# Full rows, with zeros, for the second product of each attention score, and measured prices for TensorE in the list schedule

## The chip, the cores and the metric

The kernel runs on one core of a Trainium2 chip. The metric is the device time of one execution in microseconds (us). The program is one launch; five engines (PE for matrix products, DVE and ACT for elementwise work, POOL, SP for transfers) each run their own queue in order and wait for one another by semaphores.

## The reference, cut to what matters

Two models stand one behind the other. The first block has two layers, each an attention with two kinds of heads and a gated feed-forward network (FFN). The second block has two layers with a gated linear attention, a softmax attention and a convolution branch; it isn't touched by the change but for its order. What is touched are the scores of the first block, for 256 tokens and 64-wide heads:

```python
# first kind (differential) and second kind (moba, here one block of 256 keys)
logits = jnp.einsum('bqhmd,bkhmd->bmhqk', qblk, k).astype(jnp.float32) * scale + bias
logits = jnp.where(dist >= 0, logits, -jnp.inf)
p = jax.nn.softmax(logits, axis=-1)
...
lo = jnp.einsum('bhqd,bhjd->bhqj', qch, ko).astype(jnp.float32) * scale + bias_o
```

q and k are normalised by their root mean square over the 64 channels of a head. Everything is asked for in float32.

## The kernel before, in words

**Products in parts.** The kernel keeps float32 accuracy with a faster product type by splitting each operand into a high and a low part, and multiplying high by high, high by low and low by high (`mm3`, three products for one). Weights come from HBM as `raw` tiles of 128 x 1024 numbers; ACT makes their high parts `wH`, DVE their low parts `wL`. The wide projections are the bulk of PE's work.

**Attention of the first block.** `attention1` runs four groups in each of two layers: two pairs of the first kind (`diff_pair`), two of the second (`moba_pair`). A group projects q and k for two 128-wide channel tiles, normalises them in `qk_group`, projects v, and then takes the scores in `attn_scores`, once for each of its two channel tiles `a`. A channel tile holds two heads (or two maps of one head) of 64 channels, m = 0 on partitions 0 to 63 and m = 1 on partitions 64 to 127. For token tile t (128 queries) and m there are two products into the same piece of PSUM:

- the first has all 128 rows: `qh` holds the high parts of q twice, on the head's own 64 partitions and, copied by a transfer, on the other 64; `ks` holds the high parts of k on the own partitions and the low parts on the others. One product gives high by high and high by low.
- the second takes the low parts `ql` of q, on the head's own 64 partitions only, by the high parts of k there: 64 rows.

So the eight groups of the two layers have 16 such products each, 64 first and 64 second ones in all. Between them and the transposes of the probabilities stands a chain of DVE and ACT work on `sb`: scale and bias (the bias comes from `strip`, which ACT's queue fetches by transfers in the first layer), maximum, exponential, sums, quotients.

**Order.** All instructions are recorded first (`Rec.record`), each with a price (`Rec.cost`) and a latency. `Rec.order` then simulates the engines with these prices, gives out tile slots, and the instructions are issued, engine by engine, in the order of their simulated starts. The prices decide the order of the whole kernel, not only of the part they speak of. Tiles of 512 numbers for each partition come from a ring "T" of 24 slots (`t2`, `t2r`), those of 1024 from a ring "Q" of 24 slots (`t4`, `t4r`). Ring Q holds the weights on their way (at most 4 `raw`, 7 high, 7 low), modulation weights (at most 4), and `qh` and `ks`.

Of the kernel before, what the change touches and what calls it, by code (L numbers as in the profile page):

```python
# [33 lines left out]
# columns of the packed per-channel parameters  # L34
# [79 lines left out]
# parts of the modulation (layer, part) by the tensor engine, and by the vector engine beside the FFNs and the gates  # L114
# [17 lines left out]
class Rec:  # L132
    """Records instructions, then issues them in the order of a simulated list schedule."""
# [39 lines left out]
    def cost(self, eng, method, out, args, kw):  # L173
        n = self.free(out)
        if eng == "PE":
            if method == "transpose":
                return 109
            lhs = args[1]
            m = self.free(lhs)
            if m <= 64 and self.box(out)[0] > 0:  # L180
                return 27
            if lhs.dtype == F32:
                return 2 * max(107.0, n * 0.8333 + 2)
            return max(107.0, n * 0.4167 + 2)
# [23 lines left out]
    def last(self, ap):  # L208
        """The last instruction that wrote ap's tile."""
        return max(i for _, i, w, _ in self.acc[ap.tensor.name] if w)  # L210

    def record(self, eng, method, fn, args, kw):
# [20 lines left out]
        for ap, w in [(a, False) for a in ins] + [(a, True) for a in outs]:  # L233
# [16 lines left out]
            if bank and eng == "PE" and w and (kw.get("start") or method == "transpose"):  # L250
                c = (b[0], b[1], 0, 1 << 30)   # a first product clears the bank's bits
# [19 lines left out]
    def order(self):  # L271
# [17 lines left out]
        wait = {k: sorted(v, key=lambda t: first[t]) for k, v in ftag.items()}   # tiles without slots  # L289
        held = {k: set() for k in ftag}  # L290
        freeat = {k: [0.0] * self.caps[k] for k in ftag}   # times at which free slots became free
# [3 lines left out]
        future = {e: [] for e in engs}    # (ready, prio, i)  # L295
        avail = {e: [] for e in engs}     # (prio, i)
        parked = {}                       # tag -> ops that wait for a slot
# [9 lines left out]
        def slot_time(o):  # L307
            """When the tiles that o is the first to use can have slots; None: not known yet."""
            t = 0.0
            need = {}  # L310
            for tn in o.new:
                k = self.tiles[tn]
                n = need.get(k, 0)
                fr = freeat[k]
                if len(fr) <= n or not fits(k, tn):
                    return None, k
                t = max(t, sorted(fr)[n])
                need[k] = n + 1
            return t, None

        def fits(k, tn):
            """Whether the tiles that come before tn still find slots, taken in order, when tn has one now."""
# [125 lines left out]
class Emit:  # L448
    def __init__(self, ctx, tc, io):
# [19 lines left out]
        # the tensor engine's clock rises after some time of work  # L469
# [11 lines left out]
        # weights in the order of their use  # L481
# [9 lines left out]
        for l in range(2):  # L491
            seq += [(io["w2r"][l], 1024)]
            seq += [(io["w2"][l * 66 + g], 2048) for g in range(66)]
            if l == 0:   # the output projection: once for the context, once for the latents
                seq += seq[-4:]
# [8 lines left out]
    # ---- small things  # L504
# [38 lines left out]
    # ---- weights: high and low parts of each group, split ahead of their use  # L543
# [28 lines left out]
    def psplit(self, ps, hi, lo):  # L572
        """The parts of what is in PSUM."""
# [4 lines left out]
    def mm3(self, out, w, x, start, stop):  # L578
        """out (+)= w^T x with w = (hi, lo) stationary and x = (hi, lo) moving."""
# [5 lines left out]
    def proj_t(self, out, half, x, cols):  # L585
        """out[n, tok] over the 8 k tiles; half: weights [128, 8, 128]."""
# [4 lines left out]
    def proj_v(self, out, halves, x, tok):  # L591
        """out[tok, n] over the 8 k tiles; halves: two of [128, 4, 256]."""
# [4 lines left out]
    # ---- 1/sqrt(v + eps) of columns [128, n]  # L597
# [23 lines left out]
    def gsum(self, ps, sqs, ones, start=True, stop=True):  # L621
        """Weighted sums of each [128, n] of sqs over its partitions: rows of its group of ps, one after the other."""
# [6 lines left out]
    def gcols(self, ps, ng, n):  # L629
        """The sums of ng groups token by token: a view [128, n // 128, group, row of the group] of PSUM."""  # L630
# [8 lines left out]
    def bcast(self, out, col):  # L639
        """out[:, t] = col[t] on every partition."""  # L640
        self.nc.tensor.transpose(out, col.broadcast_to([P, P]), self.ident)

    def xstat(self, j, src, state, hurry=HURRY):
        """Sums of squares over channels, gathered from channel tile j on; src [128, n]."""
# [16 lines left out]
    def xcols(self, state, n):  # L661
        """Mean squares of n tokens, token by token: columns."""
# [5 lines left out]
    def xrstd(self, state, n):  # L668
        """1/rms of n tokens, on every partition: a PSUM tile [128, n]."""
# [6 lines left out]
    # ---- modulation of the second block  # L676
# [11 lines left out]
    def mod_part(self, l, part, after):  # L688
        """512 of the 3072 modulation channels of layer l."""
# [25 lines left out]
    def mod_open(self, parts):  # L715
        """For parts by the vector engine: the silu of c along the free dimension, doubled, on every partition."""
# [16 lines left out]
    def mod_step(self):  # L733
        """The next 128 of the channels of mod_open's parts."""
# [19 lines left out]
    # ---- first block  # L754
# [13 lines left out]
    def bias_strip(self, i, after):  # L768
        """Biases of the heads 2 i and 2 i + 1 by distance."""
# [10 lines left out]
    def lam(self, l, init):  # L780
# [10 lines left out]
        # -(exp0 - exp1 + init)  # L791
# [4 lines left out]
    def xg(self, j, g, H, L):  # L796
        """The high and low parts of channel tile j of x g, not yet normalised."""
# [17 lines left out]
    def attn_scores(self, pr, a, qg, kn, rq, rcol, head):  # L815
        """Probabilities, not yet normalised, of the two 64-wide parts of channel tile a."""
# [3 lines left out]
        for t in range(2):  # L820
            for m in range(2):
                o = pss[m][:, t * T:(t + 1) * T]
                ms, qs, ks = slice(m * 64, (m + 1) * 64), slice(a * T + t * P, a * T + (t + 1) * P), slice(a * T, (a + 1) * T)
                nc.tensor.matmul(o, qg[0][:, m, qs], kn[:, m, ks], start=True, stop=False)
                nc.tensor.matmul(o, qg[1][ms, qs], kn[ms, m, ks], start=False, stop=True)
# [18 lines left out]
    def attn_transpose(self, a_sb):  # L844
# [5 lines left out]
        # blocks: (q0,k0) (q1,k0) (q1,k1)  # L850
# [3 lines left out]
    def qk_group(self, psq, psk, qscale_g, kg, guard):  # L854
        """Scaled q, normalised k and the columns 1/rms of q for two channel tiles.

        Of each 64 wide part of q its high parts twice, on all partitions, and its low parts; of k the high
        parts on the part's own partitions and the low parts on the others."""
# [10 lines left out]
        qh, ql, ks = self.t4r("qh"), self.t2r("ql"), self.t4r("ks")  # L869
        part = (slice(0, 64), slice(64, P))  # L870
        for m, own in enumerate(part):
            nc.scalar.activation(qh[own, m, :], psq[own], AF.Copy, scale=qscale_g[own])
            nc.sync.dma_start(qh[part[1 - m], m, :].bitcast(F32), qh[own, m, :].bitcast(F32))
            nc.vector.scalar_tensor_tensor(ql[own], psq[own], qscale_g[own], qh[own, m, :].bitcast(F32), ALU.mult, ALU.subtract)
# [14 lines left out]
    def attention1(self, l, H, L, Y, stat):  # L889
# [9 lines left out]
        # of each token: mean square + eps; eps times it, the guard of norms of what is not yet scaled; 1/rms  # L899
# [92 lines left out]
    def ffn(self, l, U, stat0, stat, g1):  # L992
# [6 lines left out]
        def down(i):  # L999
            w = self.nextw(2)  # L1000
            for n in range(KT):
                o = acc[n // 2][:, (n % 2) * T:(n % 2 + 1) * T]
                ns = slice(n * P, (n + 1) * P)
                for q in range(2):
# [3 lines left out]
                    # the first product clears the bits of its whole bank, so that of the other half only writes  # L1008
# [103 lines left out]
    # ---- second block  # L1112
# [21 lines left out]
    def pair_t(self, w, x, nt, nt1=None, parts=((0, 512),)):  # L1134
        """Two n tiles; their PSUM parts [128, nt]."""
# [16 lines left out]
    def group_v(self, w, x, out, order=(0, 1)):  # L1152
        """out [128 tokens, 4 token tiles, 256] for 512 tokens."""
# [6 lines left out]
    def gated(self, ps, n):  # L1160
        """2 silu(ps)."""
# [20 lines left out]
    def split4(self, t, n):  # L1182
        """The parts of t [128, 2, n of 512]."""
# [21 lines left out]
    def context0(self):  # L1205
        """The context's h of the first layer."""
# [9 lines left out]
    def layer2(self, l):  # L1216
# [6 lines left out]
        # decays' low rank part  # L1223
# [3 lines left out]
        # the columns are there twice: the products with the low parts of the second ones make rows of their own  # L1227
        nc.vector.tensor_copy(hi[:, :, 64:], lo[:, :, 64:].bitcast(F32))
        for c0, c1 in parts:
            for k in range(KT):  # L1230
                nc.tensor.matmul(ps[:, c0:c1], hi[:, k, :], h[0][:, k, c0:c1], start=k == 0, stop=k == KT - 1)
                if k < KT - 1:   # the last product has all rows, as the first
                    for q in (k,) if k < KT - 2 else (k, k + 1):
                        nc.tensor.matmul(ps[:64, c0:c1], hi[:, q, :64], h[1][:, q, c0:c1], start=False, stop=False)
        # stacked, for each direction, for one product with the stack of the decays' other factor
# [32 lines left out]
        # output  # L1268
# [22 lines left out]
    def out_last(self, l, O):  # L1291
        """The last output projection, norm and residual, with tokens on partitions."""
# [37 lines left out]
    def out_pass(self, l, s, O):  # L1330
        """Output projection, norm and residual of the latents (s = 0) or the context (s = 1)."""
# [26 lines left out]
    def h_part(self, l, s, rb, H, L):  # L1358
        """h of the latents (s = 0) or the context (s = 1)."""
# [12 lines left out]
    def pair_x(self, w, X, nt):  # L1372
        """Two n tiles of products with the 8 k tiles X."""
# [13 lines left out]
    def gate(self, l, b, X, h, nt, acc, hb, first):  # L1387
        """acc (+)= 2 sigmoid(h w_g + b_g) (X w_br), channel tile by channel tile."""
# [24 lines left out]
    def gla_head(self, l, hd, h, rz, nt):  # L1413
        nc = self.nc
        S = nt // T
        # decays: cumulated logarithms, times 16
# [7 lines left out]
        # rows for the high part, the low part, the high part again (here the low part of the weights), the low rows  # L1424
# [24 lines left out]
        # q, k, v  # L1449
# [12 lines left out]
        # products q k^T with the decays, transposed: slots (s lat0, lat1; t lat), (s ctx0, ctx1; t ctx), (s ctx0, ctx1; t lat)  # L1462
# [20 lines left out]
        for lv in (6, -1, 0, 1, 2, 3, 4, 5):  # L1483
# [6 lines left out]
            if m == 1:  # L1490
                # the factors of k are 1, those of q the single steps
# [5 lines left out]
            else:  # L1497
                # differences to the last of the first half (forward) and the first of the second half (backward)
# [26 lines left out]
        # from the context to the latents, over the state  # L1525
# [23 lines left out]
        # times v  # L1549
# [17 lines left out]
        # gate  # L1567
# [14 lines left out]
    def rope(self, t, n):  # L1582
        """Rotates the 256 latent tokens of t [128, n, 512] in place."""
# [3 lines left out]
        for b in range(4):   # the other halves of the rotated pairs; the signs are with the sines  # L1587
# [30 lines left out]
    def att_qz(self, l, i, h, nt):  # L1618
        """Two heads' q, rotated, not yet normalised; 1/rms; twice the silu of their gates."""
        nc = self.nc  # L1620
        S = nt // T
        if True:
# [10 lines left out]
            # columns: head, token tile  # L1633
# [71 lines left out]
def lay_inputs(inp):  # L1705
# [5 lines left out]
    def tpair(W, c0, c1):  # L1711
        """[128, 2 n tiles, 8 k tiles, 128]"""
# [24 lines left out]
    for l in range(2):  # L1737
# [28 lines left out]
        for part in range(6):  # L1766
            w = W[:, part * 512:(part + 1) * 512]
            if (l, part) in MODPE:   # k by k
                wada.append(w.reshape(KT, P, 512).transpose(1, 0, 2).reshape(P, 4096))
            else:   # channels on partitions  # L1770
# [107 lines left out]
```

## Time and profile before

| | |
|---|---|
| median of 3 runs | 2107.88 us (2101.41 to 2108.41) |
| span of the profiled execution | 2111.4 us |
| PE busy | 2087.5 us, 99% of the span |
| DVE busy | 1466.8 us, 69% |
| ACT busy | 1169.8 us, 55% |
| mean granted clock of PE | 0.985 of full speed |

The profiled execution has no time of its own beside its span, which lies 3.5 us above the median of the runs. Products are pipelined: one of 128 x 256 shows as 0.28 us of busy time, and the next one starts long before it ends. What a product costs PE is therefore read from the starts of its neighbours, not from its busy time.

### The profile page before, as it was taken

To read this page: it belongs to the slowest core of one execution; us is meant where nothing else is said; L and a number is where in the kernel's file an instruction comes from. 1 tells how busy PE (TensorE), PEld (TensorE's weight loads), DVE (VectorE), ACT (ScalarE), POOL (GpSimd) and SP (SyncE) were. 2 spreads that over 40 slices of the span, in tenths; PEclk is the share of its full clock that TensorE was granted. 3 is DMA by queue.
4 is the path that set the end of the run, shared out by engine and by line. 5 is a ranking of instruction groups with operands and counts; after the bars stand their busy time and mean duration, and the time that the engine had idled before them with its cause. 6 is when DMAs were issued, how large, how long until landed. Compare 5 with 4: busy or idle time off the path is not lost.

```text
span 2111.4 us, 35551 instructions
## 1 busy us (share of the span) xinstructions
PE 2087.5 (99%) x14158; PEld 1877.0 (89%) x14158; DVE 1466.8 (69%) x2846; ACT 1169.8 (55%) x2055; POOL 0.2 (0%) x4
## 2 busy tenths in 40 slices
PE   9989999999999999999999999999999999999998
PEld 7769999888999998898888888888887999999997
DVE  6668996676876689995267855554356888697664
ACT  6556555665666586764256423333356786575452
POOL 0000000000000000000000000000000000000000
PEclk9989999989999999999999999999999999999999
DMA  8565665353565512223212443333361224436552
GB/s 280 129 118 176 226 230 187 122 200 124 177 201 186 179 46 75 66 71 107 83 50 81 145 154 120 121 119 120 100 239 52 100 83 160 156 115 199 192 188 70
DMA packets 86846, 292.68 MB, mean 139 GB/s; under 512 B 9452, under 2 KB 17176, under 8 KB 86424
## 3 DMA queue, kind: packets, MB, share of 16 engines
q1 hardware_dynamic: 81544, 281.50, 39.9%
q10 hardware_dynamic: 5136, 8.91, 2.8%
q8 instruction: 111, 1.82, 0.3%
q14 instruction: 55, 0.45, 0.1%
HBM read 282.51 MB, written 4.19 MB: 136 GB/s over the span
## 4 chain that ended last, share of the span: by engine, by line
PE 97%; DMA 1%; DVE 0%; ACT 0%; issue 0%; SPq 0%; ACTq 0%; DVEq 0%
PE mm L442 76%; PE x L442 12%; PE acc L442 6%; PE ms L442 3%; DMA strip<-brow 1%; DMA xx<-in_xt_dram 0%; DVE s L442 0%; ACT h L442 0%; SPq L442 0%; DVE sb L442 0%; ACT wH L442 0%; ACT y L442 0%; ACT xg L442 0%; ACT at L442 0%; DVE h L442 0%
## 5 line engine op out<-in xcount | busy, mean ns | idle before, releaser
L442 DVE TENSOR_TENSOR wL<-raw,wH 128x1024 fp32r<-128x1024 f32 (+1 forms) x472 | 570.3, 1217 | 309.0 <-PE mm L442 146.4
L442 ACT ACTIVATE wH<-raw 128x1024 fp32r<-128x1024 f32 (+1 forms) x472 | 491.5, 1052 | 249.6 <-DVE wL L442 112.4
L442 PE MATMUL mm<-h2H,wH 128*128 128x256 f32 (+1 forms) x1504 | 504.3, 338 | 2.1 <-ACT h2H L442 2.1
L442 PE MATMUL mm<-h2L,wH 128*128 128x512 f32 (+2 forms) x1504 | 503.6, 337 | 0.0
L442 PE MATMUL mm<-h2H,wL 128*128 128x256 f32 (+1 forms) x1472 | 497.8, 338 | 0.0
L442 PEld LDWEIGHTS mm<-h2H,wH 128*128 128x128 f32 x1504 | 283.7, 190 | 33.7 <-issue 3.7
L442 PEld LDWEIGHTS mm<-h2L,wH 128*128 128x128 f32 (+1 forms) x1504 | 283.2, 189 | 28.3 <-issue 1.6
L442 PEld LDWEIGHTS mm<-h2H,wL 128*128 128x128 f32 x1472 | 279.2, 190 | 30.0 <-issue 2.2
L442 PE MATMUL mm<-h,wH 128*128 128x256 f32 x1216 | 219.6, 283 | 0.0
L442 PEld LDWEIGHTS mm<-h,wH 128*128 128x128 f32 x1216 | 189.6, 192 | 0.0
L442 PE MATMUL mm<-h,wL 128*128 128x256 f32 x608 | 171.9, 283 | 0.0
L442 PE MATMUL mm<-xg,wH 128*128 128x256 f32 x704 | 145.0, 304 | 1.9 <-ACT wH L442 1.9
L442 PE MATMUL acc<-hid,wH 128*128 128x256 f32 x704 | 128.2, 283 | 0.0
L442 PEld LDWEIGHTS mm<-xg,wH 128*128 128x128 f32 x704 | 120.3, 209 | 6.2 <-issue 3.1
L442 PEld LDWEIGHTS mm<-h,wL 128*128 128x128 f32 x608 | 116.7, 192 | 0.0
L442 PE MATMUL mm<-xL,wH 128*128 128x512 f32 (+1 forms) x320 | 111.6, 349 | 0.0
L442 PE MATMUL mm<-xH,wL 128*128 128x512 f32 (+1 forms) x320 | 111.2, 348 | 0.0
L442 PE MATMUL mm<-xH,wH 128*128 128x512 f32 (+1 forms) x320 | 111.1, 348 | 0.0
L442 PEld LDWEIGHTS acc<-hid,wH 128*128 128x128 f32 x704 | 109.7, 192 | 0.8 <-issue 0.8
L442 PE MATMUL mm<-xg,wL 128*128 128x256 f32 x352 | 106.3, 304 | 0.4 <-DVE wL L442 0.4
L442 PE MATMUL acc<-hid,wL 128*128 128x256 f32 x352 | 98.5, 283 | 0.0
L442 ACT ACTIVATE gt<-mm,hb 128x512 f32<-128x512 f32 (+1 forms) x48 | 27.8, 580 | 114.9 <-PE mm L442 114.8
(294 smaller groups left out, 3903.2 us busy)
## 6 DMA issues: line engine op xcount, KB each, us to landing
raw<-in_w_dram SPq DMA_DIRECT2D x272, 512.0 KB, 3.8
raw<-in_w1up_dram SPq DMA_DIRECT2D x88, 512.0 KB, 4.2
wada<-in_wada_dram SPq DMA_DIRECT2D x48, 512.0 KB, 5.7
raw<-in_w1in_dram SPq DMA_DIRECT2D x46, 512.0 KB, 5.2
raw<-in_w1dn_dram SPq DMA_DIRECT2D x44, 512.0 KB, 4.2
raw<-in_w1out_dram SPq DMA_DIRECT2D x16, 512.0 KB, 4.3
crow<-in_crow_dram SPq DMA_DIRECT2D x6, 512.0 KB, 6.2
qh<-qh SPq DMA_DIRECT2D x16, 128.0 KB, 2.2
```

The costliest lines, as they stand in the source:

```text
L442: o.fn(*o.args, **o.kw)
```

## The change

Three edits change what is computed or when; the rest of the diff takes comments away.

1. In `qk_group`, `ql` gets its own plane for each m, of 128 partitions x 512 numbers, in a tile of ring Q in place of one of ring T. POOL writes zeros on the other head's 64 partitions of each plane, before DVE writes the low parts on the own 64.
2. In `attn_scores`, the second product reads all 128 rows of `ql` and of `ks`. The zeros meet the low parts of k, so that the sum is the same.
3. In `Rec.cost`, PE's prices change. A product of n columns cost max(107, 0.4167 n + 2) ns and costs max(111, 0.4167 n + 13.3); a float32 one is two passes, each of twice the columns. A product with fewer than 128 rows costs 190 ns more. One with at most 32 output rows costs 110 in any case, where those with at most 64 not at the start of the partitions cost 27.

```diff
@@ Rec.cost
             lhs = args[1]
             m = self.free(lhs)
-            if m <= 64 and self.box(out)[0] > 0:
-                return 27
+            if m <= 32:
+                return 110
+            passes = 1
             if lhs.dtype == F32:
-                return 2 * max(107.0, n * 0.8333 + 2)
-            return max(107.0, n * 0.4167 + 2)
+                n, passes = 2 * n, 2
+            rows = self.box(lhs)[1] - self.box(lhs)[0]
+            return passes * max(111.0, n * 0.4167 + 13.3) + (190 if rows < P else 0)
@@ attn_scores
-                ms, qs, ks = slice(m * 64, (m + 1) * 64), slice(a * T + t * P, a * T + (t + 1) * P), slice(a * T, (a + 1) * T)
+                qs, ks = slice(a * T + t * P, a * T + (t + 1) * P), slice(a * T, (a + 1) * T)
                 nc.tensor.matmul(o, qg[0][:, m, qs], kn[:, m, ks], start=True, stop=False)
-                nc.tensor.matmul(o, qg[1][ms, qs], kn[ms, m, ks], start=False, stop=True)
+                nc.tensor.matmul(o, qg[1][:, m, qs], kn[:, m, ks], start=False, stop=True)
@@ qk_group
-        qh, ql, ks = self.t4r("qh"), self.t2r("ql"), self.t4r("ks")
+        qh, ql, ks = self.t4r("qh"), self.t4r("ql"), self.t4r("ks")
         part = (slice(0, 64), slice(64, P))
+        for m in range(2):
+            nc.gpsimd.memset(ql[part[1 - m], m, :].bitcast(F32), 0.0)
         for m, own in enumerate(part):
             nc.scalar.activation(qh[own, m, :], psq[own], AF.Copy, scale=qscale_g[own])
             nc.sync.dma_start(qh[part[1 - m], m, :].bitcast(F32), qh[own, m, :].bitcast(F32))
-            nc.vector.scalar_tensor_tensor(ql[own], psq[own], qscale_g[own], qh[own, m, :].bitcast(F32), ALU.mult, ALU.subtract)
+            nc.vector.scalar_tensor_tensor(ql[own, m, :], psq[own], qscale_g[own], qh[own, m, :].bitcast(F32), ALU.mult, ALU.subtract)
```

## Rows read from the trace of the kernel before

**Rows 1.** The page: busy time of the engines; shares of the chain that ended last.

```profile
PE 2087.5 (99%) x14158; PEld 1877.0 (89%) x14158; DVE 1466.8 (69%) x2846; ACT 1169.8 (55%) x2055; POOL 0.2 (0%) x4
...
PE 97%; DMA 1%; DVE 0%; ACT 0%; issue 0%; SPq 0%; ACTq 0%; DVEq 0%
```

**Rows 2.** Stretches: length, busy us (instructions) by engine, clock, DMA share, GB/s.

```profile
30.00:165.00 135.00, 127.06 (x780) 102.42 (x780) 86.18 (x233) 70.76 (x160) 0.00 (x0) 0.86 0.65 140
...
530.00:2111.00 1581.00, 1571.12 (x10432) 1417.81 (x10430) 1079.64 (x1960) 857.11 (x1458) 0.00 (x0) 1.00 0.38 125
300.00:320.00 20.00, 20.00 (x169) 20.00 (x169) 18.34 (x28) 12.48 (x17) 0.00 (x0) 1.00 0.76 258
```

**Rows 3.** PE's waits: for whom, us in total, times, longest.

```profile
PE x L442 <- issue: 4.8, 1, 4.8
PE x L442 <- DVE sb L442: 2.6, 2, 2.4
```

**Rows 4.** Timeline of PE around the first score burst: start, us.

```profile
35.30 0.28 PE L442 MATMUL mm<-xg,wH 128*128 128x256 f32 x1
35.42 0.28 PE L442 MATMUL mm<-xg,wL 128*128 128x256 f32 x1
...
36.78 0.39 PE L442 MATMUL x<-ks,qh 128*128 128x256 f32 x1
37.09 0.38 PE L442 MATMUL x<-ks,ql 64*128 64x256 f32 x1
37.41 0.39 PE L442 MATMUL x<-ks,qh 128*128 128x256 f32 x1
...
40.97 0.58 PE L442 MATMUL x<-ks,qh 128*128 128x256 f32 x1
41.48 0.58 PE L442 MATMUL x<-ks,ql 64*128 64x256 f32 x1
...
43.44 0.63 PE L442 MATMUL mm<-xg,wH 128*128 128x256 f32 x2
43.86 0.41 PE L442 MATMUL mm<-xg,wL 128*128 128x256 f32 x1
```

**Rows 5.** The eight score bursts, PE's products of tile ks alone: length, busy, clock.

```profile
108.70:117.75 9.05, 8.04 (x16) 0.50 0.71 24
143.00:147.52 4.52, 4.41 (x16) 1.00 0.80 26
...
498.20:503.23 5.03, 4.91 (x16) 1.00 0.34 106
sum 47.29, PE 45.02; mean PE 5.63
```

**Rows 6.** The first burst, all of PE's products.

```profile
36.15:42.00 5.85, 5.85 (x20) 0.81 0.86 81
```

**Rows 7.** The eight stretches at half clock, all of PE's products.

```profile
39.80:46.60 6.80, 6.80 (x26) 0.50 0.55 93
...
152.40:162.70 10.30, 9.45 (x31) 0.50 0.71 217
...
sum 61.60, PE 60.10; mean PE 7.51
```

**Rows 8.** The same eight stretches, products of tile ks alone.

```profile
sum 61.60, PE 18.00; mean PE 2.25
```

**Rows 9.** Timeline of PE before the third burst; the idle time stands in brackets.

```profile
108.76 0.55 PE L442 MATMUL x<-ks,qh 128*128 128x256 f32 x1 [4.75 <-issue]
```

**Rows 10.** Tile sb's waits (us, times); a row of ACT's timeline.

```profile
  DMA strip<-brow: 8.7, 4
...
95.98 8.67 ACTq L442 DMA_DIRECT2D strip<-brow  x4
```

**Rows 11.** Memsets, of DVE and of POOL.

```profile
L442 DVE MEMSET warm<- 128x512 f32 x1 | 0.5, 485 | 0.1
...
L1868 POOL MEMSET const-float32-0.0<- 128x1 f32 x1 | 0.1, 99 | 0.2 <-issue 0.2
```

## The prediction, made before the changed kernel ran

> **What bounds the kernel.** I read the page first. PE is busy for 99% of the span and carries 97% of the chain that ended last; DVE and ACT are busy for 69% and 55% [rows 1]. So whatever takes PE time counts, unless a wait takes its place. Next the stretches: the two attentions of the first block lie at about 30 to 165 us and 400 to 530 us, and in the first of them the granted clock is 0.86; from 530 us on PE is busy for 1571 of 1581 us at 1.00 [rows 2]. PE's list of waits is short, the longest one 4.8 us [rows 3]. A busy PE isn't a fast one, so I then read starts on the timeline. Two neighbouring projections of 128 x 256 start 0.12 us apart (35.30, 35.42). In the score burst a 128-row product is followed after 0.31 us and a 64-row one after 0.32 us (36.78, 37.09, 37.41), though both have 256 columns too [rows 4]. Last come the stretches at half clock, eight of them, 61.6 us together [rows 7]. The reader should see two costs that the page books as busy time: slow score products, and a clock that falls beside them.
>
> **The padding itself.** A pair of first and second product takes 0.63 us from start to start, where two projections would take 0.24 [rows 4]. The eight bursts hold 45.0 us of score products, 128 in all [rows 5]; at 0.12 us each they would take 15.4. That is 29.6 us, if what costs is the switch between 128 and 64 rows. The count of products is unchanged, and the columns of each also, so nothing is added on PE. The row that bounds it from the other side: were the rows not the cause, the gain is 0.
>
> A page of the Trainium skill speaks on either side here. "TensorEngine Tiling (Array Packing)", Key Properties, says that changing the tiling mode drains the engine; the 0.31 us beside 0.12 agrees. "TensorE: Matmul & The Clock Gate", Why this matters for your kernels, says that a product over few rows takes the same time as one over all 128: by that the padding would give 0 and the sum would be some 30 us less; the 0.31 us disagrees.
>
> **The clock.** In the first burst PE is busy for all of its 5.85 us, and the clock still falls inside it: 0.81 on the mean [rows 6], 0.50 from 39.8 to 46.6 us [rows 7]. Before it fell PE had done nothing but alternate 128 and 64 rows. The projections before the burst, one every 0.12 us, ran at full clock, as those from 300 to 320 us do [rows 2, 4]. With full rows the burst becomes like them, so I expect the clock to stay up. The eight stretches at half clock hold 60.1 us of busy PE. I leave out the one from 152.4 us (9.45 us), where PE had waited. Of the other 50.65 us, 18.0 are score products, already counted [rows 7, 8]. The remaining 32.65 us are projections at 0.21 us each (two between 43.44 and 43.86) in place of 0.12 [rows 4]: at full clock they take 32.65 x 0.12 / 0.21 = 18.65, which saves 14.0. Gross sum: 29.6 + 14.0 = 43.6 us.
>
> The same skill page, The HAM clock gate, ties half clock to an idle engine. By it a burst without a gap would not be the reason, and the 14.0 us would stay lost; the row with 5.85 busy of 5.85 us speaks against that reading.
>
> **What comes back as waits.** Three of the eight places can't give their full share.
> - The third burst begins after a PE gap of 4.75 us [rows 9], with ACT held for 8.67 us by four strip issues just before [rows 10]. Nothing in the change touches these issues. The clock is already at 0.50 through the whole burst [rows 5], and I leave it so: 16 products at 0.21 cost 3.4 us and not 1.9, and some 16 projections behind them lose 0.09 each. Back: 3.0 us.
> - The fourth burst (4.41 us) is the layer's last. After it PE runs out of projections and waits for the softmax chain, itself held by late strips for up to 8.7 us [rows 5, 10]. What the burst saves, 4.41 - 1.92 = 2.5, becomes wait. Back: 2.5 us.
> - The eighth burst (4.91 us) is the last of the second layer, without strips. It saves 3.0 us and the clock behind it some 1.5. I take half as given back: 2.3 us.
>
> The other five bursts lie between projections. In the first attention DVE is busy for 86 of 135 us [rows 2]. If all four groups there gave back their gross half of 22 us, it would be 86 of 113, or 76%. From 300 to 320 us DVE runs at 92% with PE never waiting [rows 2], so DVE's throughput holds. Its latency (scores, maximum, exponential, transposes) can show in places: between nothing and about 2 us a group (the larger wait in [rows 3] is 2.4), I take 0.6, 3.0 us in five groups. Sum of what comes back: 3.0 + 2.5 + 2.3 + 3.0 = 10.8.
>
> **POOL's zeros and ring Q.** There are 16 memsets of 64 x 512. The trace has none of this size on POOL: below stands its 0.1 us for one column, and as an upper bound I take ten times DVE's 0.485 us for 512 columns, 4.9 us [rows 11]. They need no data, only a slot, and POOL is idle for all but 0.2 us [rows 1], so either price hides. Its cover is the group's projections and the chain of norms before the scores, over 10 us; with that gone, each group would pay up to two memsets, 10 us. DVE's write to `ql` keeps its size. One tile more in ring Q takes a slot from weights on their way for a group's length. A gap for weights doesn't appear among PE's long waits now [rows 3]. I take 0, with 5 us as the upper bound: one gap like the longest.
>
> **The prices.** They reorder everything. What can be won by order outside the attentions is small: PE is idle for 9.9 us from 530 us on [rows 2]. What can be lost isn't bounded by the trace. The new price of a 256-column product, 120 ns by the formula, is the 0.12 us of the timeline; before, the formula gave 109. The plan thus comes nearer to what the chip does. I take 0, with 8 us to either side.
>
> **Sum.** 43.6 - 10.8 = 32.8, say 33 us. The profiled span of 2111.4 becomes about 2078. It lies 3.5 us above the median of the runs, which goes from 2107.9 to 2075. This kernel's measurement tells changes above some 0.5% (10.5 us) from none.
>
> **Rivals.**
> - *The chain takes it back* (0.17). The products shorten, but the clock still falls or PE waits for `sb` in every group. Then the gain is 29.6 less the 10.8, near 18 us: 2090. For it: the waits at the layer's end and the long chain between scores and transposes. Against it: PE has projections to run in between in six of eight groups.
> - *More than forecast* (0.14). The full 43.6 us come, and some of the attention's old waits go with the better plan (the 4.8 and 2.6 us): some 50 us, 2058. For it: DVE's 92% without a PE wait. Against it: the strips.
> - *The padding doesn't do what it says* (0.05). The 0.31 us come from the alternation of operands or of parts of PSUM, not from rows. Then only the order changes: 2108, within 8 us. Against it: neighbouring projections also alternate `wH` and `wL` at 0.12 us.
> - *Weights come late* (0.08). Told that a product takes longer, the planner puts the splits of weights later on DVE and ACT, and one ring slot is gone; PE then waits for `wL` where it hardly waits now. From 530 us on PE is idle for 0.6% of the time. The 33 us are used up when this rises by 2.1% of 1581 us, and the kernel is slower by over 0.5% from 2.8% (44 us): 2120. Against it: a true price makes the plan's lead true. Of this case I put 0.05 on slower and 0.03 on no change.
>
> **Chances and range.** The forecast itself, 25 to 42 us won, has 0.56: 2066 to 2083. Faster by over 0.5%: 0.56 + 0.17 + 0.14 = 0.87. Within 0.5%: 0.05 + 0.03 = 0.08. Slower: 0.05. The range runs from 2054, where the case of more ends (43.6 and 10 us), to 2097, where a chain that takes back everything but 11 us would end; it leaves out the last two rivals and the edges.
>
> **What the changed profile would show.** Right: 128 score products of 128 rows that start 0.12 us apart, with some 16 to 20 us in them in all; stretches at half clock of 10 to 25 us in place of 61.6, left only near the gap before the third burst and at the first layer's end; PE's idle time up by 5 to 10 us, on `sb` and `at`; memsets on POOL long before the burst that reads them. Wrong on the padding: starts still 0.3 us apart. Wrong on the clock: 0.50 after a burst of full rows. Wrong on the prices: PE idle for more than 20 us from 530 us on, above all for `wH` or `wL`.

## The result and the profile after

The changed kernel takes 2083.26 us (median of 4 runs, 2082.45 to 2084.66); before, 2108.14 us (4 runs). The ratio is 0.9882, with a 95% interval of 0.9868 to 0.9897: some 25 us faster, where 33 were forecast: inside the range, and at the lower edge of the forecast's own band (25 to 42). The profiled spans differ by more, 2111.4 to 2081.4. The profiled run of after took 2083.22 us with its span of 2081.4; by the same difference that of before took some 2113, which is 5 us above its median. These 5 of the 30 us are the choice of run, and they go with the clock: over the 41 runs of the kernel before that stand beside the experiments, the mean granted clock falls from 0.992 (2100.85 us) to 0.984 (2114.75 us), and the profiled run has 0.985, more half clock than the median one. All four runs of the changed kernel have 0.995.

The page of the changed kernel: busy times, shares of the chain that ended last.

```profile
PE 2052.3 (99%) x14158; PEld 1856.1 (89%) x14158; DVE 1467.0 (70%) x2846; ACT 1173.6 (56%) x2055; POOL 8.5 (0%) x20
...
PE 81%; DVE 6%; ACT 4%; issue 2%; DMA 0%; DVEq 0%; ACTq 0%
```

The count of products is the same as in [rows 1] and PE's busy time has fallen by 35 us. The chain that ended last isn't PE's alone any more: DVE and ACT have 10% of it, so in places PE now waits for them.

PE's timeline in the first burst, and the score products (tile ks) of the bursts (length, busy, clock):

```profile
36.08 0.28 PE L444 MATMUL x<-ks,qh 128*128 128x256 f32 x1
36.20 0.28 PE L444 MATMUL x<-ks,ql 128*128 128x256 f32 x1
36.32 0.28 PE L444 MATMUL x<-ks,qh 128*128 128x256 f32 x1
```

```profile
36.00:38.00 2.00, 1.92 (x16) 1.00 0.97 126
...
98.90:102.40 3.50, 3.40 (x16) 0.50 0.78 26
128.80:132.40 3.60, 3.46 (x16) 0.50 0.86 73
...
458.50:460.80 2.30, 2.15 (x16) 1.00 0.68 224
sum 21.10, PE 19.71; mean PE 2.46
```

The starts are 0.12 us apart where [rows 4] has 0.31, and 45.0 us of score products [rows 5] have become 19.7. Six of the eight bursts run at full clock. The two others begin behind a gap of PE, whose waits are these, with ACT's row just before the first of them:

```profile
PE x L444 <- issue: 9.3, 2, 5.7
PE x L444 <- DVE fL L444: 2.3, 4, 0.9
PE x L444 <- DVE F L444: 2.3, 4, 0.6
```

```profile
84.69 8.49 ACTq L444 DMA_DIRECT2D strip<-brow  x3
```

The stretches at half clock from 30 us on, PE's products:

```profile
97.10:104.00 6.90, 5.00 (x23) 0.51 0.79 26
127.90:134.70 6.80, 5.76 (x27) 0.50 0.88 90
```

These two, 13.7 us, answer to 61.6 in [rows 7]. Beside them, 3.4 us at half clock lie at the very start, and the last 4.5 us of the span come behind PE's last product.

Where the time went is read from one product: `mm<-h2H,wH` stands in the second block alone, and its row gives the start of its first and of its last one. Before, then after:

```profile
L442 PE MATMUL mm<-h2H,wH x1504: 276/339/506, 726.6 to 2078.1; 128*128 128x256 f32 x96, 128*128 128x512 f32 x92
```

```profile
L444 PE MATMUL mm<-h2H,wH x1504: 274/353/504, 682.7 to 2048.0; 128*128 128x256 f32 x96, 128*128 128x512 f32 x92
```

The second block begins 43.9 us earlier, and its products take 1365.3 us from first to last in place of 1351.5. So the first block won 43.9 us, about the gross sum of the prediction (some 5 of it by the choice of run, since the half clock of [rows 7] lies there), and the second, none of whose instructions was changed, gave back 13.8. PE's timeline shows how, before and after, at the same place of the first linear attention head:

```profile
787.00 1.13 PE L442 MATMUL x<-F 128*128 128x128 f32 x8
787.89 0.48 PE L442 MATMUL mm<-h2H,wH 128*128 128x512 f32 x1
788.20 1.06 PE L442 MATMUL x<-F 128*128 128x128 f32 x8
789.02 0.48 PE L442 MATMUL mm<-h2L,wH 128*128 128x512 f32 x1
```

```profile
744.71 1.13 PE L444 MATMUL x<-F 128*128 128x128 f32 x8 [0.64 <-DVE F L444]
746.46 1.13 PE L444 MATMUL x<-F 128*128 128x128 f32 x8 [0.61 <-DVE F L444]
```

A set of eight small products needs factors `F` that DVE and ACT make. Before, projections stand between the sets and cover the wait. After, the sets follow one another and each waits: 1.75 us from set to set, of which 0.6 shows as idle and the rest lies under the modelled end of the product before.

Over the whole second block PE's idle time rises only from 1.9 to 6.6 us, a third of the 13.8. An estimate from the starts of all its products gives the rest: the time between two starts beyond 0.4167 n + 13 ns (n the columns of the first) sums to 35.8 us before and 49.6 after, and 10.1 of these 13.8 us stand before products of `F`, `fH` and `fL`, the factors of the linear attention.

### The profile page after: what moved, and what is told of

The parts are those of the page before. It is cut to its first block, busy times and chain, and to the rows that moved or that the text cites. A ratio compares the mean times of both kernels' runs of the same rounds, so it can differ in the third digit from the quotient of the medians.

```text
span 2081.4 us, 35662 instructions
## 1 busy us (share of the span) xinstructions
PE 2052.3 (99%) x14158; PEld 1856.1 (89%) x14158; DVE 1467.0 (70%) x2846; ACT 1173.6 (56%) x2055; POOL 8.5 (0%) x20
## 4 chain that ended last, share of the span: by engine, by line
PE 81%; DVE 6%; ACT 4%; issue 2%; DMA 0%; DVEq 0%; ACTq 0%
PE mm L444 65%; PE x L444 8%; PE acc L444 6%; PE ms L444 2%; DVE g L444 1%; DVE F L444 1%; ACT e L444 1%; ACT wH L444 0%; DVE att L444 0%; ACT h L444 0%; DVE s L444 0%; ACT L444 0%; DVE fL L444 0%; DVE bE L444 0%; DVE h L444 0%
## 5 line engine op out<-in xcount | busy, mean ns | idle before, releaser
L444 PE MATMUL mm<-xg,wH 128*128 128x256 f32 x704 | 134.4, 288 | 1.7 <-ACT wH L444 1.7
L444 PEld LDWEIGHTS mm<-xg,wH 128*128 128x128 f32 x704 | 112.1, 194 | 5.0 <-issue 2.8
L444 PE MATMUL mm<-xg,wL 128*128 128x256 f32 x352 | 101.7, 290 | 0.2 <-DVE wL L444 0.2
L444 PE MATMUL mm<-wL,h2H 128*128 128x256 f32 x320 | 91.1, 285 | 0.0
```

Of the source, the lines that this page charges most:

```text
L444: o.fn(*o.args, **o.kw)
```

## The experiments

In the tables and sentences below, "first block" is the start of the first `mm<-h2H,wH`, "second block" the time from there to the start of its last one, as above.

### Rows or prices: e1, e2

e1 is the changed kernel with PE's old prices:

```diff
-            if m <= 32:
-                return 110
...
-            return passes * max(111.0, n * 0.4167 + 13.3) + (190 if rows < P else 0)
+            if m <= 64 and self.box(out)[0] > 0:
+                return 27
+            if lhs.dtype == F32:
+                return 2 * max(107.0, n * 0.8333 + 2)
+            return max(107.0, n * 0.4167 + 2)
```

> The changed kernel with PE's old prices: full rows, zeros by POOL and the tile in ring Q stay. Theory A (the rows pay, the prices cost): the first block keeps its gain of about 44 us, and the second block, laid out by the old prices, doesn't lose the 14 us that it lost with the change: 2060 to 2070 us, faster than the changed kernel (2083). Theory B (the true prices lay out the first block better and give part of its gain, and the second block loses for another reason, such as the tile in ring Q or the different moment at which it begins): 2083 to 2095 us, with the loss of some 14 us behind 683 us still in the trace.

e2 is the kernel before with the third edit alone.

> The kernel before with the new prices alone: 64-row second products, priced 190 ns more. Theory A: the score bursts and their half clock stay as before, and the second block loses its 14 us: 2115 to 2125 us, slower than before (2108). Theory B: the first block gains some 10 us by its order and the second loses nothing: 2095 to 2105 us.

| | median us | ratio to before, 95% | first block | second block |
|---|---|---|---|---|
| before | 2108.14 | | 726.6 | 1351.5 |
| changed | 2083.26 | 0.9882, 0.9868 to 0.9897 | 682.7 | 1365.3 |
| e1, rows only | 2079.10 | 0.9870, 0.9855 to 0.9885 | 692.5 | 1352.9 |
| e2, prices only | 2117.76 | 1.0051, 1.0039 to 1.0064 | 717.5 | 1365.4 |

```profile
L442 PE MATMUL mm<-h2H,wH x1504: 277/364/506, 692.5 to 2045.4; 128*128 128x256 f32 x96, 128*128 128x512 f32 x92
```

```profile
L444 PE MATMUL mm<-h2H,wH x1504: 274/348/504, 717.5 to 2082.9; 128*128 128x256 f32 x96, 128*128 128x512 f32 x92
```

The prices alone cost the second block 13.9 us; the rows alone cost it 1.4. That part of theory A holds. Its number for e1 was missed by 9 us, since its first block ends at 692.5 and not near 683. The two first blocks part in the first layer: with full rows and old prices the fourth burst begins at 138.8 us, with new ones at 128.9. So the new prices do win some 9 us in the first block, as theory B said, and lose more in the second. Neither theory was whole. (e2's first block is 9.1 us shorter than before, but some 6 of these are the choice of run: by the medians e2 loses 11 us, where its second block loses 13.9.) e2 waits for `F` and `fL` as the changed kernel does, 2.3 and 2.2 us; before and e1 have no such wait.

### Which prices: e3, e4

e3 has full rows, the old rules and the new constants for wide products; e4 has full rows, the old price for these and the new one for small and float32 products. Both edits are shown against the old rules:

```diff
# e3
-            return max(107.0, n * 0.4167 + 2)
+            return max(111.0, n * 0.4167 + 13.3)
# e4
-            if m <= 64 and self.box(out)[0] > 0:
-                return 27
+            if m <= 32:
+                return 110
             if lhs.dtype == F32:
-                return 2 * max(107.0, n * 0.8333 + 2)
+                return 2 * max(111.0, n * 0.8333 + 13.3)
```

> Full rows with the old rules for float32 products and for products of few output rows, and only the price of the wide products raised (0.4167 n + 13.3, at least 111). If the wide price makes the second block's order worse: 2078 to 2086 us, as the changed kernel. If the prices of the small products do it: 2060 to 2070 us, as full rows with the old prices.

> Full rows with the old price of the wide products and the new prices for float32 products and for those of at most 32 output rows (110 ns). If the small prices make the second block's order worse: 2075 to 2086 us. If the wide price does it: 2060 to 2070 us.

e3 took 2086.36 us (0.9903, 0.9888 to 0.9918), e4 2083.99 (0.9895, 0.9878 to 0.9912). First e3, then e4, each with PE's wait for `F`:

```profile
L442 PE MATMUL mm<-h2H,wH x1504: 276/338/481, 690.3 to 2051.3; 128*128 128x256 f32 x96, 128*128 128x512 f32 x92
...
PE x L442 <- DVE F L442: 2.4, 5, 0.6
```

```profile
L442 PE MATMUL mm<-h2H,wH x1504: 274/384/499, 684.6 to 2047.8; 128*128 128x256 f32 x96, 128*128 128x512 f32 x92
...
PE x L442 <- DVE F L442: 0.7, 2, 0.4
```

The second block takes 1361.0 and 1363.2 us. Either group of prices loses most of the 13.8 us by itself, so neither expectation told them apart: it isn't one price. They don't lose it in the same places. e3 waits for `F` as the changed kernel does; e4 hardly does, and by the same estimate from starts only 3.9 of its 11.7 us (4.6 of 9.5 in e3) stand before products of `F`, `fH` and `fL`. That each move away from the old prices upsets an order that happened to fit is the reading that is left; it isn't shown.

### Prices by block: e6

The new prices for what is recorded before the second block, the old ones behind it:

```diff
+        self.true_prices = True          # in Rec.__init__
...
+            if not self.true_prices:
+                (the old rules)
...
+        nc.true_prices = False           # at the head of block2
```

> The changed kernel with the new prices for the first block's instructions and the old ones for the second block's. Theory A (the second block lost its 14 us by the new prices of its own instructions, and the first layer's 8 us more than with full rows alone came from the new prices there): the first block ends near 682 us as in the changed kernel, and the second takes as long as before within 2 us: 2064 to 2071 us, faster than both the changed kernel (2083) and full rows alone (2079). Theory B (the one plan can't be cut in two: the second block loses because of the state in which it begins): 2078 to 2086 us.

2072.19 us (2070.10 to 2072.55), ratio 0.9832, 0.9811 to 0.9853: faster than both kernels, and 1 us above the expected band.

```profile
L451 PE MATMUL mm<-h2H,wH x1504: 274/364/582, 683.3 to 2037.5; 128*128 128x256 f32 x96, 128*128 128x512 f32 x92
```

First block 683.3, second 1354.2, which is 2.7 above before and 1.3 above e1. The first block's gain and the second block's loss can be had apart, so the state in which the second block begins isn't what costs it.

### The switch between 128 and 64 rows: e5, e9

If the switch costs, and not the 64 rows, then 64-row products may stay if they switch half as often. Both runs start from the kernel before, with its old prices; e9 adds the line on `nc.after`, which tells the planner of an order:

```diff
-            for m in range(2):
-                ... first product of m, second product of m
+            for m in range(2):
+                nc.tensor.matmul(os[m], qg[0][:, m, qs], kn[:, m, ks], start=True, stop=False)
+            nc.after = len(nc.ops) - 1       # e9 alone
+            for m in range(2):
+                ms = slice(m * 64, (m + 1) * 64)
+                nc.tensor.matmul(os[m], qg[1][ms, qs], kn[ms, m, ks], start=False, stop=True)
```

> The kernel before, with 64-row second products and the old prices, but with the four products of a token tile in another order: both first products, then both second ones, which stand on different halves of the rows. The switches between 128 and 64 rows are halved, 64 to 32 round trips. Theory A (the switch costs): a set of four takes about 0.64 us in place of 1.26 (0.12, 0.21, 0.00, 0.31, by starts of the kernel before), the score products some 20 us in all in place of 45, and with the bursts shorter half clock behind them becomes rarer: 2072 to 2088 us. Theory B (a 64-row product is slow by itself, or two products into one PSUM piece are): the score products stay near 40 to 45 us: 2100 to 2110 us.

e5: 2100.56 us (0.9972, 0.9955 to 0.9990), the score products 41.6 us by the stretch from 30 to 530 us. The planner had taken most sets apart again (first, second, first, second at 0.31 us each), so the run (theory B's band, 2100 to 2110) tells little.

> The kernel before, with 64-row second products and the old prices; now the planner is told that the two second products of a token tile come after both first ones, so that all 32 sets of four stand in the order first, first, second, second. Theory A (the switch between 128 and 64 rows costs, not the 64 rows): a set takes some 0.64 to 0.74 us in place of 1.26, the score products 20 to 24 us in all in place of 45 (41 in the run whose sets the planner took apart), half clock behind the bursts becomes rarer, and the time is 2075 to 2092 us. Theory B (64-row products are slow by themselves): the score products take 35 us or more, 2095 to 2108 us.

e9: 2082.35 us (0.9885, 0.9868 to 0.9901), the score products 27.2 us by the same stretch (45.5 before, 21.1 in the changed kernel). PE's timeline:

```profile
37.03 0.28 PE L442 MATMUL x<-ks,qh 128*128 128x256 f32 x1
37.24 0.38 PE L442 MATMUL x<-ks,ql 64*128 64x256 f32 x2
37.55 0.50 PE L442 MATMUL x<-ks,qh 128*128 128x256 f32 x2
37.98 0.38 PE L442 MATMUL x<-ks,ql 64*128 64x256 f32 x2
38.30 0.39 PE L442 MATMUL x<-ks,qh 128*128 128x256 f32 x1
```

A set of two first and two second products takes 0.75 us (37.55 to 38.30) in place of 1.26, and the two 64-row ones of a set start together (a row of two lasts 0.38 us, as one alone does). Theory A's time holds, at 3 us above its band for the products. With no zeros at all, e9 is as fast as the whole change; beside e1, which has the same old prices, its first block ends at 693.1 in place of 692.5.

The 0.75 us alone doesn't show that the switch costs and not the 64 rows: since the two 64-row products run together, a set holds half as many switches and also half as many stretches of 64-row work. What tells more is the first 128-row product behind a switch, here a projection:

```profile
39.37 0.39 PE L442 MATMUL x<-ks,ql 64*128 64x256 f32 x2
39.68 0.38 PE L442 MATMUL mm<-xg,wH 128*128 128x256 f32 x1
39.91 0.28 PE L442 MATMUL mm<-xg,wL 128*128 128x256 f32 x1
40.02 0.40 PE L442 MATMUL mm<-xg,wH 128*128 128x256 f32 x2
```

It is followed after 0.23 us (39.68 to 39.91), the next one after 0.11. A 128-row product that comes from 128 rows and is followed by 64 takes 0.21 (37.03 to 37.24). Neither has few rows, so about half of what a round trip costs beyond two projections (0.63 - 0.24 = 0.39 us) is the switch. The other half lies on the step from the 64-row product to the next (0.31 in place of 0.12), and no run separates the switch from the 64 rows there: no trace has two 64-row products on the same half in a row. The 0.1 us behind the switch is also what makes a set 0.75 us and not the expected 0.64.

In e9 no burst lowered the clock:

```profile
30.00:92.00 62.00, 58.57 (x440) 1.00 0.80 195
141.00:500.00 359.00, 355.77 (x2847) 1.00 0.58 193
```

Between and behind these stretches it fell three times (92.8, 130.4 and 1577.6 us), each time beside a gap of PE.

### The gaps that stay: e7, e8, e10, e11, e12

Each changes only who issues the twelve transfers of the six bias strips, or when, on top of e6 (the diff puts the edits together):

```diff
-            nc.scalar.dma_start(st[:, a * T:(a + 1) * T], win)
+            nc.sync.dma_start(...)           # e7, e11; nc.gpsimd in e8
...
-                    for i in ((pr,) if kind == 0 else (2 + 2 * pr, 3 + 2 * pr)):
+                    for i in (((0, 1), (2, 3)), ((4, 5), ()))[kind][pr]:      # e10, e11
+                    g = 4 * kind + 2 * pr                                     # e12
+                    self.bias_strip(g, mark)
+                    self.bias_strip(g + 1, the v projection's last op)
```

> As the run with prices split by block, with the twelve bias strips issued by SP in place of ACT. Theory A (ACT held by its own strip issues makes the gaps before the third and fourth score burst and the half clock that follows them): the gap before the third burst, 5.7 us in the changed kernel, and most of the 13.6 us at half clock go, and 5 to 10 us are won: 2056 to 2064 us. Theory B (the strips' transfers are slow whoever issues them, and the weights behind them on SP wait): PE waits for strips or weights in place of ACT, and the time stays within 4 us of the run with split prices, or rises.

> As the run before, with the strips issued by POOL, whose queue holds the memsets of the zeros and nothing else. Theory A: nothing waits behind the strips on that queue but the zeros of the next group, so that 5 to 10 us are won as with SP, or more than with SP if there the weights wait. Theory B: the strips land as late as from ACT, and the softmax of the first layer's last group waits for them as before: within 4 us of the run with split prices.

> Prices split by block, the strips issued by ACT as before, but each group of the first layer issues those of the next one, so that they have a group's length (some 25 us) to land. Theory A (the strips come late, wherever they are issued): the gaps before the third and fourth burst (5.7 and 4.7 us with split prices) and the waits for strips go, 6 to 14 us are won on split prices (2072): 2058 to 2066 us. Theory B (what costs is ACT held while it issues): the hold of some 8 us moves with the issues and stops ACT a group earlier: 2066 to 2075 us.

> As the run with early strips, issued by SP. Theory A: as with ACT, 2058 to 2066 us, since neither the landing nor the hold of ACT is left; the two waits for sb of 17 us in all that SP's strips made without the earlier issue go. Theory B (the strips' transfers crowd out the weights): PE waits for weights in the first layer, 2070 to 2080 us.

> Prices split by block, the strips issued by ACT; each of the first three groups issues one strip (two transfers) at its start, as before, and one more only behind its v projection, so that no four issues stand in a row and each strip but the first has about a group's length to land. Theory A (two transfers in a row are issued in about 1.2 us, four in a row hold their engine for 8 to 9 us, and this hold makes the gaps before the bursts): the gaps of 5.5 and 4.4 us of split prices (2072) go, with the half clock behind them, and 6 to 14 us are won: 2058 to 2066 us. Theory B (the transfers behind one another are slow however they are spaced): ACT is still held for several us in each of the three groups, as with early strips, and the time is 2072 to 2082 us.

| | median us | ratio to before, 95% |
|---|---|---|
| e6, ACT, in the group | 2072.19 | 0.9832, 0.9811 to 0.9853 |
| e7, SP | 2076.91 | 0.9857, 0.9836 to 0.9878 |
| e8, POOL | 2085.28 | 0.9895, 0.9874 to 0.9917 |
| e10, ACT, a group early | 2081.58 | 0.9882, 0.9867 to 0.9897 |
| e11, SP, a group early | 2088.68 | 0.9914, 0.9899 to 0.9929 |
| e12, ACT, spread | 2072.05 | 0.9835, 0.9817 to 0.9854 |

None is faster than e6; e12 equals it. Theory A's band was missed by all five. Theory B's took in e7 (4.7 us slower than e6) and e12; e8, e10 and e11 came out slower than either theory said. With SP, ACT isn't held, but SP is, and the weights behind the strips come late (ACT waits 10.9 us for them); SP's timeline of e7:

```profile
78.77 8.87 SPq L451 DMA_DIRECT2D strip<-brow  x4
87.73 4.91 SPq L451 DMA_DIRECT2D raw<-in_w1in_dram  x1
```

POOL issues four in 2.1 us, but then SP's own transfers are held, one of q for 10.6 us (0.5 in e6 at the same place) and two of weights for 19.0; POOL's and SP's timelines of e8:

```profile
70.88 2.12 POOL L451 DMA_DIRECT2D strip<-brow  x4
```

```profile
78.58 10.59 SPq L451 DMA_DIRECT2D qh<-qh  x1
89.31 19.03 SPq L451 DMA_DIRECT2D raw<-in_w1in_dram  x2
```

PE then waits 24.9 us for `ks`. Issued a group early by ACT (e10), no engine waits for a strip to land, but each of three groups now issues four in a row and holds ACT for 7 to 9 us. Issued early by SP (e11), strips hold SP twice for over 9 us, and PE waits 13.8 us for `sb` and 14.2 us before a score burst. Spread (e12), only the first group still issues four in a row; ACT's timeline of e12:

```profile
32.80 0.62 ACTq L451 DMA_DIRECT2D strip<-brow  x1
33.46 9.07 ACTq L451 DMA_DIRECT2D strip<-brow  x3
66.55 1.20 ACTq L451 DMA_DIRECT2D strip<-brow  x2
70.83 0.53 ACTq L451 DMA_DIRECT2D strip<-brow  x1
71.40 3.73 ACTq L451 DMA_DIRECT2D strip<-brow  x1
...
102.25 3.12 ACTq L451 DMA_DIRECT2D strip<-brow  x1
```

Here two in a row take 1.2 us, four hold the engine for over 9, and some 4 us of distance leave 3 to 4 us of that. In e12 the waits for strips are gone, and PE reaches the fourth burst 3.7 us later than in e6 although its first burst begins 6.2 us later (44.0 us), behind the first group's own four issues. So both theories have a part: four in a row hold longest, as A said, but ACT is still held in each of three groups (9.1, 3.7 and 3.1 us) and the time is B's. Strips also land slowly whoever issues them and however spaced, 7.2 to 18.1 us after their issue in e12 and 7.1 to 25.5 in e8, where four in a row land some 5 us apart (at 78.0, 82.9, 87.9 and 92.7 us). A version with the second strip of the first group issued later wasn't tried.

## Why the prediction was right

- **The padding (29.6 us gross).** Right. Starts 0.12 us apart, 45.0 to 19.7 us, 25.3 won. Of the 4.3 us that are missing, 3.0 are the clock: two bursts at half clock (3.4 and 3.5 us), one of them forecast. The rival that the padding doesn't do what it says falls, since the operands and the parts of PSUM alternate as before and only the rows have changed. That it is the switch, and not a 64-row product by itself, e9 shows for about half of the cost; the padding removes both.
- **The clock (14.0 us).** Right in its mechanism: 61.6 us at half clock became 13.7, and what stays begins behind gaps of PE. No burst of full rows lowered the clock: in all ten kernels with full rows and in e9, each stretch at half clock between 30 us and PE's last product begins beside a gap of PE (1.8 to 24.9 us), while in before, e2 and e5 some begin inside score bursts without one. The size was read from a run with more half clock than most and then taken from the median: some 5 of the 8 us by which 33 was too much.
- **What comes back as waits (10.8 us).** Right in the sum for the old order, and in part by luck. With rows alone (e1) the first block ended 34.1 us earlier by the profiled spans, where the sum gave 32.8 (some 29 by the medians: 27 in all and 1.4 lost behind). But up to the fifth burst, which begins at 401.0 us before and at 388.8 in e1, only 12 were won, where the prediction's terms give 22.3 less 6.7, some 16; from there on 22 were won, where they give 21.4 less 4.1, some 17. So the first layer, where strips held the third and fourth burst as the prediction named them, gave back more than its terms, and the second nothing. The waits on `sb` and `at` that were to show are 0.6 us in the changed kernel.
- **POOL's zeros and ring Q (0).** Right. A memset takes 0.52 us, between the bounds of 0.1 and 4.9, and no wait of PE is put down to POOL: the first zeros come at 0.7 us, and the nearest end 5 us before DVE's write to their tile. Weights don't come later for the slot in ring Q: PE's waits for `wH` and `wL` are 1.9 us, 2.3 before.

```profile
L444 POOL MEMSET ql<- 64x512 f32 x16 | 8.3, 521 | 399.8 <-PE acc L444 259.7 <-PE x L444 55.3 <-PE mm L444 49.9
```

- **The prices (0, with 8 us to either side).** This is the term that was mis-sized, and in both directions at once: 9.8 us won in the first block (692.5 to 682.7), 13.8 lost in the second against 1.4 without them. The step that failed in it is the sentence that the plan comes nearer to what the chip does. The price of the wide products did (120 ns by formula and by starts); the order that followed from it was worse in the second block (e3), where projections no longer cover DVE's factors. The rival on late weights named the loss in the right place but by the wrong engine's work: none of PE's waits over 0.5 us behind 683 us is for `wH` or `wL`. The prediction's own sign for this term, PE idle for more than 20 us from 530 us on, didn't fire: it is 14.3 us (9.9 before), since most of the loss lies under busy time.

Terms by rows: 34.1 + 9.8 = 43.9 in the first block, less 13.8, gives the 30 us of the profiled spans; less 5 for the choice of run, the 25 of the medians. So it is partly luck that the sum came near: the prices won 9.8 us in one block and cost 12.4 in the other. That the wide price and the small prices each cause most of the loss is measured; which choice of the planner follows from which price stays open, and so does where e4 lost it.

## What to carry to other kernels

Read starts, not busy time, on an engine that is 99% busy: 45 us of it were 15 us of work, and the rest switches and a clock at half. Before a gain read from one profile is taken from a median, compare that run's granted clock with the others'. Either give all products of a burst the same rows, or put those with few rows side by side so that the shape changes seldom. When a planner's prices are corrected, measure each stage of the kernel by itself, since an order can lose cover that no single price speaks of, and keep old prices where they planned better.

## What the runs showed of the hardware that was not expected

- The half clock behind a score burst came with PE busy throughout [rows 6], and went when the same count of products ran with equal rows: 0.985 to 0.995 on the mean of the span. It also went in e9, with 64-row products and half the switches.
- Two 64-row products on different halves of the rows start together (both at 37.98 us in e9's timeline: the row of two lasts 0.38 us, as one alone, and the next product starts 0.32 us later).
- A switch between 128 and 64 rows shows on the 128-row products on either side of it: 0.21 us before and 0.23 us behind it, in place of 0.12.
- Four strip transfers in a row, each reading windows of one partition's row, hold their issuer for 4 to 9 us on ACT and on SP. POOL isn't held, but SP's other transfers then are, two of them for 19 us.
